# Output stage of a streaming encoder step: matmuls taken by tile and piece, and another order of column groups for the first tile

## The chip, the cores and the metric

One core of a Trainium2 chip runs the whole kernel. The metric is the device time of one execution in microseconds (us), lower is better. The engines are named as the profile names them: PE is TensorE (matmuls), PEld its weight loads, DVE is VectorE, ACT is ScalarE, POOL is GpSimd, SP is SyncE, whose queue issues nearly all DMA transfers. Each engine works through its own list of instructions in the order of that list.

## The reference, cut to what matters

The kernel computes one layer for 1024 prompt rows and 64 sample rows, 1024 columns wide, all in 32-bit floats: a normalised projection, eight heads of forgetting attention, four heads of attention to memory tokens, a pooling mixer, gates on all three, one output projection, and a last normalisation. The change concerns the last three steps alone:

```python
    cat = jnp.concatenate([
        jax.nn.silu(gf) * fox_o.reshape(B, S, FOX_W),
        jax.nn.silu(gp) * pool_o,
        jax.nn.silu(gm) * mem_o.reshape(B, S, MEM_W)], axis=-1)
    return x + cat @ w_out
...
    y_prompt = rmsnorm(hp, g_final)
    y_sample = rmsnorm(hs, g_final)
```

`cat` has 1024 columns, `w_out` is 1024 x 1024. The row norm at the end needs all 1024 columns of a row before any of them can be scaled.

## The kernel before, in words

**Two-part numbers.** Every product is built from 32-bit operands that are split in a high and a low part: high times high, high times low, low times high. So a product over 1024 rows of `w_out` is 8 steps of 128 rows (k = 0 to 7) with three matmuls each, 24 in all. For the 64 sample rows the high and the low part of `cat` lie side by side in one 128-column stationary operand, so a product takes 16 matmuls there, and the upper half of its result is added on afterwards (the copy `ysl`).

**Tiles and pieces.** The output stage goes over nine row tiles in the order `order = (8, 0, 1, ..., 7)` (line 1213): first the 64 sample rows (t = 8, here "the first tile"), then the prompt rows in tiles of 128. For each tile `out_prep(t)` (line 1150) loads the attention results and the gates, multiplies them and splits the product into `chi` (ACT) and `clo` (DVE); it does so in two halves, k = 0 to 3 and k = 4 to 7, for the prompt tiles. `out_tile(t)` (line 1248) then multiplies by the columns of `w_out` in three column groups: group 0 is columns 0 to 511, group 1 is 512 to 767, group 2 is 768 to 1023. One piece is one tile by one group: a run of 24 (or 16) matmuls, 512 or 256 columns wide. Groups 1 and 2 share one accumulator, so the three pieces fill two banks. The list `steps` (lines 1260 to 1263) gives the order in which the pieces are written down; two pieces that share an accumulator stay in that order, a piece in the other accumulator may pass them. When an accumulator is full, DVE adds the input rows `xt` to it, ACT squares the sum and adds it up, and after the second one DVE and ACT work out the row norm, scale the row and store it. The last tile (t = 7) uses three accumulators and does this per piece.

**Accumulators and buffers.** The tiles take the four PSUM rings in turn (line 1268): the first tile has `pp`, t = 0 has `s`, t = 1 has `pt`, t = 2 has `o`, t = 3 again `pp`, and so on up to t = 6 with `o` and t = 7 with `pp` and, for its third piece, `s`. In the trace the accumulator's name therefore tells the tile. `chi` and `clo` have room for three tiles in all, and two of the three places are those of the weights of the last projections. `xt` has two buffers: the third tile's rows are loaded when the first tile's rows have been stored.

**W_out.** `load_wout` (line 1219) brings the groups in the order 1, 0, 2, because it puts them where the three chunks of the normalised input lay, and these come free in that order as the last projections end. Each group is loaded, copied to a high part `wh` (ACT) and a rest `wl` (DVE or POOL), in two steps for a group of 256 columns and four for group 0.

**The order of the work.** All operations are first written down in a list with what they depend on. A planner (`Planner.flush`, line 190) then runs through them with a cost for each: at every step it takes, per engine, the operation with the smallest key of line 219,

```python
                    key = (t + late, op.rank, -op.level, op.seq)
```

where `t` is the earliest time at which that operation can start by the planner's own clock, `rank` is 0 for the output stage's matmuls, and `level` is the length of the longest chain of work that hangs on it. The result is the fixed list of each engine. Once several operations of PE can start at once, `rank` decides and then `level`; between tiles whose levels run close together the choice goes back and forth. All instructions are issued from line 252, so the trace is read by tile names and not by lines.

Of the kernel before, what the change touches and what calls it, by code (L numbers as in the profile page):

```python
# [42 lines left out]
class Planner:  # L43
# [5 lines left out]
    def __init__(self, nc, tc):  # L49
        self.nc, self.tc = nc, tc  # L50
        self.ops = []
        self.acc = {}
        self.slots = {}
        self.alloc = {}
        self.users = {}
        self.home = {}
        self.free = {e: 0.0 for e in self.ENG}
        self.lock = {"vector": 0.0, "gpsimd": 0.0}
        self.mode = self.table = None
        self.calm = self.boost = False  # L60
        self.dma = [0.0] * 16
        for e in self.ENG:
            setattr(self, e, _Eng(self, e))
# [31 lines left out]
    def add(self, eng, fn, args, kw):  # L95
        op = Op()
        op.eng, op.fn, op.args, op.kw = eng, fn, args, kw
        op.seq, op.succ, op.npred, op.ready, op.level = len(self.ops), [], 0, 0.0, 0.0
        op.mode = op.table = op.start = op.bytes = None
        op.port = False  # L100
        aps = [(i == 0, a) for i, a in enumerate(args)] + [(k in self.OUTS, a) for k, a in kw.items()]
        aps = [(w, a) for w, a in aps if hasattr(a, "tensor")]
        writes = [a for w, a in aps if w]
        reads = [a for w, a in aps if not w]
        self.cost(op, writes, reads)
        homes = {self.home.get(a.tensor.name) for a in writes + reads}
        into = {self.home.get(a.tensor.name) for a in writes}
        urgent = into & {"ps", "pt", "po"} if eng == "tensor" else "pp" in homes or "wp" in into
        op.rank = -1 if self.boost or urgent and not self.calm else 0
        preds = set()  # L110
        for w, a in aps:
            name, p0, p1, f0, f1 = self.box(a)
            hist = self.acc.setdefault(name, [])
            keep = []
            for h in hist:
                hw, q0, q1, g0, g1, o = h
                hit = q0 <= p1 and p0 <= q1 and g0 <= f1 and f0 <= g1
                if hit and (w or hw) and o is not op:
                    preds.add(o)
                if not (w and hit and p0 <= q0 and q1 <= p1 and f0 <= g0 and g1 <= f1) or o is op:  # L120
                    keep.append(h)
            keep.append((w, p0, p1, f0, f1, op))
            self.acc[name] = keep
            self.users.setdefault(name, []).append(op)
        for o in preds:
            self.link(o, op)
        self.ops.append(op)
        return op
# [144 lines left out]
def tile_hymba_step(  # L273
# [6 lines left out]
    nc = Planner(tc.nc, tc)  # L280
# [16 lines left out]
    def nm(s):  # L297
        uid[0] += 1
        return f"{s}_{uid[0]}"
# [10 lines left out]
    def row(name):  # L310
        return rp.tile([P, 512], F32, tag="row", name=nm(name))
# [65 lines left out]
    def quarter_ms(out, ss):  # L377
        nc.vector.tensor_scalar(out, ss, 0.25 / D, 0.25 * EPS, op0=ALU.mult, op1=ALU.add)

    def rsqrt(out, ms, pool):  # L380
        m, n = ms.shape
        t = pool.tile([P, 4], F32, tag="rsb", name=nm("rt"))[:m, :n]
        nc.scalar.activation(t, ms, AF.Sqrt)
        nc.vector.reciprocal(out, t)
        if n == 1:
            nc.vector.scalar_tensor_tensor(out, out, ms, t, op0=ALU.mult, op1=ALU.add)
        else:
            nc.vector.tensor_tensor(out, out, ms, op=ALU.mult)
            nc.vector.tensor_tensor(out, out, t, op=ALU.add)
        nc.vector.reciprocal(out, out)  # L390
# [41 lines left out]
    def mm3(acc, trip, n):  # L432
        for i, (l, r) in enumerate(trip):
            mm(acc, l, r, i == 0, i == n - 1)
# [378 lines left out]
    def small(shape, tag):  # L813
        return ap_.tile(shape, F32, tag=tag, name=nm(tag), bufs=6)
# [23 lines left out]
    def nbt(n):  # L838
        tag, w = ("nb", 512) if n <= 512 else ("nc", NPR)
        return ap_.tile([P, w], F32, tag=tag, name=nm(tag))  # L840

    def ptile(n=1024):
        tag, w, bufs = ("P", 512, 4) if n <= 512 else ("Q", 1024, 3)
        return ap_.tile([P, w], F32, tag=tag, name=nm(tag), bufs=bufs)
# [368 lines left out]
    order = (8, 0, 1, 2, 3, 4, 5, 6, 7)  # L1213
# [34 lines left out]
    def out_tile(t):  # L1248
        m = P if t < 8 else NSA
        c = slice(t * P, t * P + m)  # L1250
        if t not in prep:
            prep[t] = out_prep(t)
        xt_ = ap_.tile([P, NT + PAST], F32, tag="ks", name=nm("xt"))[:, :D]
        nc.sync.dma_start(xt_[:m], xn[c, :])
        xt = [xt_[:, :512], xt_[:, 512:]]
        ch, cl = prep[t]
        end = t == order[-1]
        ss = small([P, 4], "ss")
        xg = ptile() if end else None
        if end:  # L1260
            steps = [(0, 0, 0, 512, True), (1, 1, 0, 256, True), (2, 2, 0, 256, True)]
        else:
            steps = [(1, 2, 256, 256, False), (0, 0, 0, 512, True), (1, 1, 0, 256, True)]
        accs = {}
        prev = None
        for pi, pc, o, w, full in steps:
            if pi not in accs:
                ring = (ppt, pst, ptt, otile)[order.index(t) % 4]
                accs[pi] = ring() if pi < 2 else (pst if ring is ppt else ppt)()
            acc = accs[pi]  # L1270
            trip = []
            for k in range(KT):
                trip += [(ch[:, k, :], whi[pc][:, k, :w]), (ch[:, k, :], wlo[pc][:, k, :w])]
                if t < 8:
                    trip.append((cl[:, k, :], whi[pc][:, k, :w]))
            mm3(acc[:, o : o + w], trip, len(trip))
            if not full:
                continue
            n = w if end else 512
            c0 = (0, 512, 768)[pi]  # L1280
            x_ = xt[min(pi, 1)][:m, (0, 0, 256)[pi] : (0, 0, 256)[pi] + n]
            if t == 8:
                tt_ = row("ysl")
                nc.scalar.copy(tt_[:m], acc[m:, :])
                nc.vector.tensor_tensor(x_, tt_[:m], x_, op=ALU.add)
            nc.vector.tensor_tensor(x_, acc[:m, :n], x_, op=ALU.add)
            sp_ = ss[:m, pi : pi + 1]
            sq = nbt(512)
            nc.scalar.activation(sq[:m, :n], x_, AF.Square, accum_out=sp_)
            if prev is None:  # L1290
                quarter_ms(sp_, sp_)
            else:
                nc.vector.scalar_tensor_tensor(
                    sp_, sp_, 0.25 / D, prev, op0=ALU.mult, op1=ALU.add
                )
            prev = sp_
            if end:
                nc.vector.tensor_tensor(xg[:, c0 : c0 + n], x_, gfb[0][:m, c0 : c0 + n], op=ALU.mult)
        r = small([P, 1], "fr")
        rsqrt(r[:m], ss[:m, pi : pi + 1], ap_)  # L1300
        for nh in (0, 1):
            cols = slice(nh * 512, nh * 512 + 512)
            if not end:
                nc.vector.scalar_tensor_tensor(
                    xt[nh][:m], xt[nh][:m], r[:m], gfb[0][:m, cols], op0=ALU.mult, op1=ALU.mult
                )
                nc.sync.dma_start(y_o[c, cols], xt[nh][:m])
            elif nh:
                nc.vector.tensor_scalar(xg[:, cols], xg[:, cols], r, None, op0=ALU.mult)
                nc.sync.dma_start(y_o[c, cols], xg[:, cols])  # L1310
            else:
                nc.scalar.activation(xg[:, cols], xg[:, cols], AF.Copy, scale=r)
                nc.scalar.dma_start(y_o[c, cols], xg[:, cols])
# [64 lines left out]
    for t in order:  # L1378
        out_tile(t)
# [109 lines left out]
```

## Time and profile before

| what | value |
|---|---|
| median of 3 runs | 590.33 us (590.27 to 591.16) |
| the profiled execution's own time | 590.34 us |
| span of that execution, first to last instruction | 588.5 us |
| mean granted clock of TensorE | 0.996 of full speed |
| PE busy | 561.2 us (95% of the span), 3623 matmuls |
| DVE, ACT, POOL busy | 349.1, 299.1 and 249.8 us (59%, 51% and 42%) |
| DMA | 126.33 MB, mean 215 GB/s |

The span is what the trace covers; 1.84 us of the execution's own time lie outside it. Busy shares are means over stages with different limits. The output stage is the last 112 us or so of the span.

### The profile page before, as it was taken

Reading aid. Unit: us, or ns where it says so; the run is one execution under the profiler, and the core shown is the slowest. Engines: PE = TensorE matmul, PEld = TensorE weight load, DVE = VectorE, ACT = ScalarE, POOL = GpSimd, SP = SyncE. Lnnn points to the kernel's source line nnn. Section 1 sums busy time; section 2 is a strip of 40 time slices with the busy share of each in tenths; the row PEclk is TensorE's granted clock in tenths of the full one; section 3 lists DMA queues with packets and bytes.
Section 4 is the critical chain, followed back from the end, with each engine's and each line's share of the span. In section 5 each row is a group of like instructions: output and inputs, shape, how many; then the busy total and the mean of one; then the engine's idle time right before and its main releaser. Section 6 shows DMA issues by size and latency. Waiting matters only on the chain.

```text
span 588.5 us, 10778 instructions
## 1 busy us (share of the span) xinstructions
PE 561.2 (95%) x3623; PEld 504.3 (86%) x3623; DVE 349.1 (59%) x822; ACT 299.1 (51%) x675; POOL 249.8 (42%) x358
## 2 busy tenths in 40 slices
PE   7799999999999999999999999999999989999993
PEld 5789999888979889988988889889898867989983
DVE  5774431112788877756798965864356374656334
ACT  5564631121677877767886864862234243323202
POOL 2301464353774544434479851522323394322200
PEclk9999999999999999999999999999999999999998
DMA  8998753658997896596687897735256337577541
GB/s 301 312 339 298 229 174 117 242 202 281 281 349 242 291 280 189 154 322 210 213 238 269 274 263 235 210 125 152 76 152 187 113 109 195 142 231 213 159 143 72
DMA packets 96448, 126.33 MB, mean 215 GB/s; under 512 B 30434, under 2 KB 68618, under 8 KB 94858
## 3 DMA queue, kind: packets, MB, share of 16 engines
q1 hardware_dynamic: 96106, 125.39, 66.6%
q8 instruction: 29, 0.48, 0.3%
q10 hardware_dynamic: 288, 0.27, 0.1%
q14 instruction: 25, 0.20, 0.1%
HBM read 86.41 MB, written 39.21 MB: 213 GB/s over the span
## 4 chain that ended last, share of the span: by engine, by line
PE 76%; DMA 10%; DVE 6%; issue 3%; POOL 3%; ACT 1%; SPq 0%; DVEq 0%; POOLq 0%; ACTq 0%
PE pp L252 40%; PE s L252 13%; PE o L252 11%; PE pt L252 11%; DMA nat<-in_xn_dram 5%; POOL wl L252 2%; DMA nc<-gpd 2%; DMA nc<-gsd 1%; DMA catd<-cat 1%; DVE s L252 1%; DMA xr<-in_xT_dram 1%; DVE Q L252 1%; DVE ot L252 1%; DVE phl L252 1%; SPq L252 0%
## 5 line engine op out<-in xcount | busy, mean ns | idle before, releaser
L252 PE MATMUL pp<-xh,whi 128*128 128x320 f32 (+2 forms) x480 | 149.9, 335 | 2.8 <-DVE gr L252 1.1
L252 PE MATMUL pp<-xl,whi 128*128 128x320 f32 (+2 forms) x480 | 148.0, 331 | 0.0
L252 PE MATMUL pp<-xh,wlo 128*128 128x512 f32 (+2 forms) x480 | 147.7, 332 | 0.0
L252 PEld LDWEIGHTS pp<-xh,whi 128*128 128x128 f32 x480 | 88.1, 188 | 11.6 <-DVE gr L252 2.3
L252 POOL TENSOR_TENSOR wlo<-wr,whi 128x512 fp32r<-128x512 f32 (+2 forms) x44 | 60.1, 1384 | 86.7 <-ACT whi L252 75.1
L252 PEld LDWEIGHTS pp<-xh,wlo 128*128 128x128 f32 x480 | 88.1, 188 | 6.9
L252 PEld LDWEIGHTS pp<-xl,whi 128*128 128x128 f32 x480 | 88.1, 188 | 6.5
L252 DVE TENSOR_TENSOR phl<-pt,phl 128x512 fp32r<-128x512 f32 (+1 forms) x96 | 60.4, 642 | 11.9 <-ACT phl L252 10.8
L252 ACT CAST phl<-pt 128x512 fp32r<-128x512 f32 (+1 forms) x96 | 51.8, 550 | 25.0 <-PE pt L252 18.4
L252 POOL TENSOR_TENSOR cat<-ot 64x256 f32<-64x256 f32 x48 | 36.1, 754 | 55.6 <-DVE ot L252 33.0
L252 PE MATMUL o<-phl,vs 128*128 128x512 f32 (+1 forms) x160 | 55.3, 416 | 0.0
L252 PE MATMUL pt<-ident,Q 128*128 128x128 f32 x248 | 47.6, 272 | 1.9 <-DVE phl L252 1.8
L252 ACT CAST whi<-wr 128x1024 fp32r<-128x1024 f32 (+1 forms) x25 | 24.6, 982 | 45.2 <-PE pp L252 43.0
L252 ACT ACTIVATE Q<-Q,m 128x576 f32<-128x576 f32 (+4 forms) x40 | 38.0, 950 | 17.4 <-DVE m L252 17.1
L252 DVE TENSOR_TENSOR ot<-o,ot 64x512 f32<-64x512 f32 x48 | 32.8, 685 | 13.4 <-ACT ot L252 12.8
L252 PEld LDWEIGHTS pt<-ident,Q 128*128 128x128 f32 x248 | 32.1, 140 | 7.2 <-issue 2.2
L252 PE MATMUL s<-ks,qb 128*128 128x512 f32 (+3 forms) x128 | 37.4, 374 | 0.0
L252 POOL TENSOR_TENSOR P<-P,P 128x512 f32<-128x512 f32 (+2 forms) x17 | 18.5, 1096 | 41.8 <-DMA P<-catd 23.3
L252 ACT COPY ot<-o 64x512 f32<-64x512 f32 x48 | 27.9, 581 | 11.8 <-PE o L252 9.1
L252 PEld LDWEIGHTS o<-phl,vs 128*128 128x128 f32 x160 | 27.8, 190 | 3.3 <-DVE ot L252 0.2
L252 DVE CUSTOM_DVE_ANT_0 Q<-s,nc 128x512 f32<-128x512 f32 (+2 forms) x40 | 24.0, 599 | 10.9 <-PE s L252 6.0
L252 DVE TENSOR_TENSOR gr<-pp,rb 128x512 f32<-128x512 f32 (+2 forms) x24 | 12.5, 532 | 26.8 <-PE pp L252 25.8
(250 smaller groups left out, 1330.2 us busy)
## 6 DMA issues: line engine op xcount, KB each, us to landing
qd<-hl SPq DMA_DIRECT2D x24, 576.0 KB, 4.7
wr<-in_wt_dram SPq DMA_DIRECT2D x20, 512.0 KB, 4.2
qa<-qd SPq DMA_DIRECT2D x12, 640.0 KB, 5.7
ks<-kd SPq DMA_DIRECT2D x8, 800.0 KB, 6.4
qb<-qd SPq DMA_DIRECT2D x12, 512.0 KB, 5.0
P<-catd SPq DMA_DIRECT2D x17, 256.0 KB, 3.0
nat<-in_xn_dram SPq DMA_DIRECT2D x8, 512.0 KB, 8.1
kd<-hl SPq DMA_DIRECT2D x16, 256.0 KB, 5.1
```

The source lines that it names most:

```text
L252: getattr(getattr(self.nc, op.eng), op.fn)(*op.args, **op.kw)
```

## The change

Every operation of PE that `out_tile` writes down gets as its rank three times the place of its tile in the order, plus the place of its piece in `steps`. The rank stands ahead of the level in the planner's key, and behind the time. Ranks of other engines and of the earlier stages stay as they are. Besides, the first tile gets its own list of pieces: group 1, then group 0, then group 2, where it had 2, 0, 1 as the other tiles have.

```diff
         self.calm = self.boost = False
+        self.turn = None
...
         op.rank = -1 if self.boost or urgent and not self.calm else 0
+        if self.turn is not None and eng == "tensor":
+            op.rank = self.turn
...
         if end:
             steps = [(0, 0, 0, 512, True), (1, 1, 0, 256, True), (2, 2, 0, 256, True)]
+        elif t == order[0]:
+            steps = [(1, 1, 0, 256, False), (0, 0, 0, 512, True), (1, 2, 256, 256, True)]
         else:
             steps = [(1, 2, 256, 256, False), (0, 0, 0, 512, True), (1, 1, 0, 256, True)]
...
-        for pi, pc, o, w, full in steps:
+        for si, (pi, pc, o, w, full) in enumerate(steps):
+            nc.turn = 3 * order.index(t) + si
```

A step is (accumulator, column group, first column in the accumulator, width, whether the accumulator is full after it). Nothing is added to or taken from what is computed.

## Rows read from the trace of the kernel before

**Rows 1.** The profile's page, the chain of work that ended last: shares of the span by engine.

```profile
PE 76%; DMA 10%; DVE 6%; issue 3%; POOL 3%; ACT 1%; SPq 0%; DVEq 0%; POOLq 0%; ACTq 0%
```

**Rows 2.** Busy time by stretch of the span. Columns: stretch, its length, busy us (and instructions) of PE, PEld, DVE, ACT, POOL, granted clock of PE, DMA share, GB/s.

```profile
476.00:488.50 12.50, 8.47 (x33) 5.33 (x31) 8.62 (x12) 4.75 (x8) 11.20 (x10) 1.00 0.45 145
488.50:579.00 90.50, 90.49 (x594) 82.47 (x594) 44.41 (x95) 22.82 (x55) 21.66 (x28) 1.00 0.57 168
579.00:588.50 9.50, 0.00 (x0) 0.00 (x0) 5.12 (x20) 2.79 (x11) 0.00 (x0) 0.74 0.30 110
```

**Rows 3.** PE's timeline from the end of the last projection on. Columns: start us, duration us, engine, operation, accumulator and operands, shape, count, and in brackets the idle time before it and what ended it.

```profile
476.55 0.50 PE L252 MATMUL s<-wh,chi 128*128 128x512 f32 x1 [0.43 <-ACT chi L252]
...
478.31 0.50 PE L252 MATMUL s<-wh,clo 128*128 128x512 f32 x1 [1.02 <-DVE clo L252]
...
479.11 0.39 PE L252 MATMUL pp<-wh,chi 128*128 128x512 f32 x1
...
483.51 0.50 PE L252 MATMUL pp<-wl,chi 128*128 128x512 f32 x1 [0.56 <-POOL wl L252]
...
484.92 0.50 PE L252 MATMUL pp<-wl,chi 128*128 128x512 f32 x1 [0.69 <-POOL wl L252]
...
487.55 0.50 PE L252 MATMUL pt<-wh,chi 128*128 128x512 f32 x1 [1.20 <-ACT chi L252]
```

**Rows 4.** The timelines of DVE, POOL and ACT in the same stretch: when the parts of W_out and of the first tiles' operands were made.

```profile
461.29 2.89 POOL L252 TENSOR_TENSOR wl<-nc,wh 128x512 fp32r<-128x512 f32 x2 [4.31 <-ACT wh L252]
...
478.17 0.68 DVE L252 SCALAR_TENSOR_TENSOR chi<-P,chi 128x512 fp32r<-128x512 f32 x1
...
481.73 3.14 POOL L252 TENSOR_TENSOR wl<-wr,wh 128x512 fp32r<-128x512 f32 x2
...
486.38 0.58 ACT L252 COPY ysl<-pp 64x512 f32<-64x512 f32 x1 [6.50 <-PE pp L252]
486.87 0.63 ACT L252 ACTIVATE chi<-P 128x512 fp32r<-128x512 f32 x1
...
491.21 1.22 DVE L252 TENSOR_TENSOR wl<-wr,wh 128x1024 fp32r<-128x1024 f32 x1 [0.24 <-ACT wh L252]
```

**Rows 5.** PE's timeline where the matmuls run without a gap: two 512 wide on one accumulator, the first and the last of eleven 256 wide on one accumulator, and two 256 wide on alternating accumulators with 17 others between them.

```profile
480.92 0.40 PE L252 MATMUL s<-wh,clo 128*128 128x512 f32 x1
481.15 0.40 PE L252 MATMUL s<-wh,chi 128*128 128x512 f32 x1
...
493.18 0.28 PE L252 MATMUL pp<-wh,chi 128*128 128x256 f32 x1
...
494.38 0.28 PE L252 MATMUL pp<-wh,chi 128*128 128x256 f32 x1
...
500.07 0.28 PE L252 MATMUL s<-wh,clo 128*128 128x256 f32 x1
...
502.17 0.28 PE L252 MATMUL s<-wh,clo 128*128 128x256 f32 x1
```

**Rows 6.** All engines at the end of the span, in order of time: the last matmuls of t = 6 (`o`) and of t = 7 (`s`), and the work behind them up to the last stores.

```profile
577.54 0.28 PE L252 MATMUL o<-wh,clo 128*128 128x256 f32 x1
...
578.71 0.28 PE L252 MATMUL s<-wh,clo 128*128 128x256 f32 x1
...
579.40 0.41 DVE L252 TENSOR_TENSOR xt<-s,xt 128x256 f32<-128x256 f32 x1
...
580.28 0.40 ACT L252 ACTIVATE nb<-xt 128x256 f32<-128x256 f32 x1
580.59 0.19 ACT L252 ACTIVATION_READ_ACCUMULATOR nb<-xt 128x1 f32 x1
...
581.12 0.15 DVE L252 SCALAR_TENSOR_TENSOR ss<-ss 128x1 f32<-128x1 f32 x1
...
581.31 0.20 ACT L252 ACTIVATE rt<-ss 128x1 f32<-128x1 f32 x1 [0.44 <-DVE ss L252]
...
581.86 0.15 DVE L252 RECIPROCAL fr<-rt 128x1 f32<-128x1 f32 x1
...
582.30 0.22 DVE L252 RECIPROCAL fr<-fr 128x1 f32<-128x1 f32 x2
582.50 0.72 ACT L252 ACTIVATE Q<-Q,fr 128x512 f32<-128x512 f32 x1 [0.99 <-DVE fr L252]
582.56 1.42 DVE L252 SCALAR_TENSOR_TENSOR xt<-xt,fr,gfb 128x512 f32<-128x512 f32 x2
...
583.89 0.48 DVE L252 TENSOR_SCALAR Q<-Q,fr 128x512 f32<-128x512 f32 x1
584.40 0.62 SPq L252 DMA_DIRECT2D out_dram<-Q  x1
```

**Rows 7.** Two of the last stretches of the span, columns as in rows 2: the first in which the last stores moved data, and the one in which nothing moved any more.

```profile
584.00:584.40 0.40, 0.00 (x0) 0.00 (x0) 0.38 (x1) 0.00 (x0) 0.00 (x0) 0.50 0.63 241
...
587.20:588.50 1.30, 0.00 (x0) 0.00 (x0) 0.00 (x0) 0.00 (x0) 0.00 (x0) 0.50 0.00 0
```

**Rows 8.** ACT and DVE in the middle of the stage: the first tile's second evacuation, the second half of t = 2's operands, and DVE's wait for the input rows of t = 1, whose releaser is the store of the first tile's rows out of the same buffer.

```profile
499.62 0.59 ACT L252 COPY ysl<-pp 64x512 f32<-64x512 f32 x1 [2.65 <-PE pp L252]
...
509.38 0.69 DVE L252 SCALAR_TENSOR_TENSOR clo<-P,chi 128x512 fp32r<-128x512 f32 x1 [0.37 <-ACT chi L252]
...
516.80 1.29 DVE L252 TENSOR_TENSOR xt<-pt,xt 128x512 f32<-128x512 f32 x2 [3.19 <-DMA out_dram<-xt]
```

## The prediction, made before the changed kernel was run

> **What bounds the kernel now.** I read the views from the coarse to the fine. The chain of work that ended last says that PE is the engine to look at: 76% of the span [rows 1]. The busy time by stretch says where in the output stage PE is not the limit. From 488.5 to 579.0 us it is busy for 90.49 of 90.50 us, at a granted clock of 1.00, which is the 2.4 GHz level; there only fewer matmuls would help. Before that, from 476.0 to 488.5, it is busy for 8.47 of 12.50 us, so 4.03 us are idle. After it, from 579.0 to 588.5, it does nothing for 9.5 us [rows 2]. The reader is to keep these two holes in mind, 4.0 and 9.5 us, since an order of matmuls can change only them.
>
> The PE timeline shows what fills the first hole. PE starts on `s` (t = 0) at 476.55, waits 1.02 us for `clo`, begins the first tile (`pp`) at 479.11, and then waits for the rest of group 0 of W_out (`wl`, 0.56 and 0.69 us) and 1.20 us for the operands of t = 1 [rows 3]. All of these matmuls are 512 wide: group 0. The timelines of the helpers say why no other group is used. Group 1 is complete at 464.18 (461.29 + 2.89), group 0 only at 484.87, group 2 at 492.44 [rows 4]. But group 1 stands behind group 2 in `steps`, in the same accumulator, so what was ready first waits for what comes last.
>
> The timeline of all engines shows the second hole: t = 6 (`o`) ends at 577.54 + 0.28 = 577.82 and t = 7 at 578.71 + 0.28 = 578.99, only 1.2 us later [rows 6]. Both evacuations then stand on DVE and ACT at once, with PE idle.
>
> **Part 1: the first tile takes group 1 first.** It adds and removes no instruction. It moves 16 matmuls of 256 columns from behind 492.44 into the first hole. One such matmul follows another after 0.12 us (493.18 to 494.38 is ten steps); on alternating accumulators it is (502.17 - 500.07) / 18 = 0.117 us, so changing accumulators costs nothing and saves nothing [rows 5]. 16 x 0.1175 = 1.9 us. The first tile's operand is ready at 478.17 + 0.68 = 478.85 [rows 4]. From there to 487.55, where t = 1 begins, are 8.7 us. Work to be placed there: 16 matmuls of the first tile on group 0 and the 7 of t = 0 that are left of its first twelve, each 0.23 us (480.92 to 481.15) [rows 5], which is 5.4 us, and now 1.9 us more: 7.3 of 8.7. So it fits. It can't all fall where PE idles today: the first tile's last matmuls still wait for `wl` at 484.87, and PE keeps the planned order, so up to 0.7 us (the wait at 484.92 [rows 3]) may be lost to a matmul of `s` planned on the wrong side of a wait. The bounds are 1.2 and 1.9 us; I take 1.9, since by rank the seven of `s` come behind the first tile and so fill exactly its waits.
> Behind 487.55 the supply is as it was: the second half of t = 0, then group 2 at 492.44. No wait on W_out is added, since group 2 now stands third, not first, for the first tile. ACT's `ysl` at 486.38 and the `chi` behind it at 486.87 [rows 4] keep their place, as group 0 ends when it did.
>
> **Part 2: matmuls by tile and piece.** Again no instruction comes or goes, on PE or on a DMA queue: weight loads are one per matmul in both orders. Each prompt tile now runs as one block: 24 x 0.23 + 48 x 0.1175 = 11.2 us. In the full stretch this changes nothing by itself. At the end, t = 6 is finished 11.2 us before the last matmul, and the first two pieces of t = 7 are finished 5.6 and 2.8 us before it, so their evacuation lies beside matmuls. What is left after the last matmul is one piece of 256 columns. From the durations and the start distances of [rows 6], with 0.04 us from PE to DVE or between DVE and ACT and 0.07 us into the square: add 0.04 + 0.41, square and its accumulator 0.07 + 0.50, `ss` 0.04 + 0.15, root 0.04 + 0.20, then to the last reciprocal 0.04 + 0.44 (581.86 to 582.30) and to the scaling 0.20 (582.30 to 582.50): 2.13 us, and then DVE's half 0.48 and ACT's half 0.72 side by side. The product with `gfb` (0.4 us on DVE) fits beside the square. So SP's last store is issued at 2.64 us after the last matmul and ACT's at 2.85, where today SP's goes out at 584.40, which is 5.41 us after it [rows 6]. The reason is in the same rows: today the two scalings of t = 6 (582.56, 1.42 us) stand before that of t = 7, and their adds and sums before its.
> From the last issue to the end of the span it takes 588.5 - 584.40 = 4.1 us today. Data moves from about 584.1 to 587, and nothing in the last 1.3 us [rows 7]: four stores of 256 KB (128 x 512 x 4 bytes) in 2.8 us. With two stores left it is 1.4 us of data. One bound keeps the 4.1 us: a tail of 2.85 + 4.1 = 7.0 us, 2.5 saved. The other takes 0.8 us from issue to first data, 1.4 us of data and 1.5 us to the end: 2.64 + 3.7 = 6.4, 3.1 saved. I take the middle, 2.8 us, since some of the 4.1 us is the queue of the other two stores, but not all.
>
> **The cover that strict order gives up.** Mixed tiles always have other matmuls at hand; in strict order a late operand stops PE. The nearest place is t = 2: its second half's `clo` is finished at 509.38 + 0.69 = 510.07 today [rows 8]. In strict order, group 2 is complete at 492.44, then follow the rest of t = 0 on group 0, the first tile's group 2 (ending near 495.7), two pieces of t = 0 and the three of t = 1 less the half done at 491: t = 2 starts near 509.7 and needs k = 4 at 511.1. The first tile leaves PE at 495.7 instead of 499.6 [rows 8], which frees its operand's place and its evacuation 3.9 us sooner, so that `clo` should come near 506. Slack 5 us; later tiles have 22 us for each preparation. Cost taken: 0; bounds 0 and 4.2 us per boundary (next part).
> The trace shows mixing as full cover, 0.01 us idle in 90.5 [rows 2]. The Trainium skill, page "Perfetto Trace Analysis", section "Optimization Strategy", says that where the contended engine changes over time, interleaving the regimes may help; by it, un-mixing is the wrong direction, and the rival right below gives the time. In this stage the contended engine is PE in all tiles alike, so the trace bears it out only for the two holes.
>
> **Sum.** 590.34 - 1.9 - 2.8 = 585.6 us against the profiled execution's own time; the median, 590.33, is the same number. Its own range: 585.0 (2.0 and 3.3 saved) to 586.6 (1.2 and 2.5).
>
> **Rivals.**
> *DVE holds the operands back (slower).* The first tile's store must be done before t = 1's input rows are loaded into its `xt`; today DVE waits 3.19 us for that, until 516.80, at the add for t = 1 [rows 8]. Strict order finishes the first accumulator of t = 1 near 507, while the rows come only 3.9 us sooner, near 512.9. If the planner, whose clock differs from the chip's, put that add ahead of t = 2's `clo`, this would be ready at 512.9 + 1.3 + 0.7 = 514.9 or later, 3.8 to 4.2 us after PE wants it. One such stall gives 590.34 - 4.7 + 4.2 = 589.8, no change; two, at t = 2 and at t = 3, give 590.34 - 4.7 + 8.4 = 594.0. It decides from 4.7 us of idle PE between 488.5 and the last matmul. For it: the wait exists today. Against it: the planner counts that load too, and it orders by when things are ready.
> *The first hole stays.* The planner's clock has the first tile's operand later than the chip, so `s` goes first and the new matmuls end behind 487.55: only the tail's 2.8 us, 587.5.
> *The tail stays long.* The last two tiles part, but the end hangs on stores and on small operations in the same order: 0.5 us instead of 2.8 saved at the end, 587.9. Against it: SP's last store can't wait for t = 6 any more.
> *It doesn't do what it says.* If matmuls are ready one at a time, `t` decides and rank never does: 590.3. Against it: 594 matmuls in 90.5 us without a gap, so many are ready at once [rows 2].
>
> **How the numbers follow.** Forecast 0.64; first hole stays 0.12; tail stays long 0.09; one stall or no effect 0.07; two stalls or more 0.08. A change below 0.2% (1.2 us) can't be told from none here. Faster: 0.64 + 0.12 + 0.09 = 0.85; same 0.07; slower 0.08. The range goes from 584.7, a little below the forecast's own lower end for what the sums leave out, to 588.6, which takes in the second and third rival.
>
> **What would show it.** Right: between 476 and 488.5 PE is busy about 10.3 us instead of 8.47, with `pp` 256 wide right after 479; in the full stretch runs of 24 on one accumulator, and no idle; the last `o` 11 us before the last matmul; about 6.7 us from that matmul to the end of the span. Wrong: idle PE at a change of tile with `clo` or `chi` as its releaser, DVE waiting for `xt` longer than 3.2 us, or a last store issued later than 3.5 us after the last matmul.

## The result, and the profile after

The changed kernel takes 584.55 us, the median of 3 runs (584.19 to 586.34), beside 590.33 us before: a ratio of 0.9914 with a 95% interval of 0.9888 to 0.994. The forecast was 585.6 us in a range of 584.7 to 588.6: the median lies 0.15 us below the lower end, while the ratio, taken of 590.33, gives 585.3 us, inside it. The span of the profiled execution is 582.8 us, against 588.5.

Busy time by stretch of the changed kernel, columns as in [rows 2]:

```profile
476.00:488.50 12.50, 10.24 (x51) 8.08 (x51) 7.76 (x9) 4.43 (x9) 10.17 (x9) 1.00 0.48 143
488.50:573.00 84.50, 84.50 (x549) 76.77 (x548) 49.42 (x103) 23.56 (x58) 21.69 (x27) 1.00 0.62 183
573.00:582.80 9.80, 3.20 (x28) 3.00 (x26) 3.05 (x10) 1.95 (x6) 0.00 (x0) 0.91 0.14 54
```

In the first 12.5 us PE is busy for 10.24 us where [rows 2] had 8.47. Part of that is the window: the stage begins 1.26 us earlier here, and in a window moved by as much (474.74 to 487.24) PE is busy for 9.81 us. The long stretch is still without a gap. The last stretch holds the end of PE's work and what follows it. PE's timeline, which answers to [rows 3], shows what fills the first hole:

```profile
475.29 0.51 PE L255 MATMUL s<-wh,chi 128*128 128x512 f32 x1 [0.42 <-ACT chi L255]
...
477.04 0.50 PE L255 MATMUL s<-wh,clo 128*128 128x512 f32 x1 [1.01 <-DVE clo L255]
...
477.83 0.28 PE L255 MATMUL pp<-wh,chi 128*128 128x256 f32 x1
...
479.62 0.28 PE L255 MATMUL pp<-wl,chi 128*128 128x256 f32 x1
...
486.43 0.50 PE L255 MATMUL pt<-wh,chi 128*128 128x512 f32 x1 [1.20 <-ACT chi L255]
```

Sixteen `pp` matmuls of 256 columns stand where the first tile used to begin with group 0, and the two waits for `wl` (0.56 and 0.69 us) are gone. The wait for `chi` of t = 1 stays at 1.20 us. The chain of waits (start, length, what) then shows each tile as one block of 72 matmuls, 11.2 to 11.3 us, and at the end 24 matmuls of the last piece:

```profile
508.61 11.29 PE o L255 x72
519.90 11.28 PE pp L255 x72
...
553.67 11.29 PE o L255 x72
564.95 8.43 PE pp L255 x48
573.38 2.84 PE s L255 x24
```

The last `o` (t = 6) now ends at 553.67 + 11.29 = 564.96, 11.2 us before the last matmul; in [rows 6] it was 1.2 us. The timeline of all engines behind the last matmul, which answers to [rows 6]:

```profile
575.92 0.28 PE L255 MATMUL s<-wh,clo 128*128 128x256 f32 x1
576.24 0.42 DVE L255 TENSOR_TENSOR xt<-s,xt 128x256 f32<-128x256 f32 x1 [1.60 <-PE s L255]
...
576.76 0.42 ACT L255 ACTIVATE nb<-xt 128x256 f32<-128x256 f32 x1 [2.31 <-DVE xt L255]
...
578.38 0.72 ACT L255 ACTIVATE Q<-Q,fr 128x512 f32<-128x512 f32 x1 [0.68 <-DVE fr L255]
578.38 0.49 DVE L255 TENSOR_SCALAR Q<-Q,fr 128x512 f32<-128x512 f32 x1
578.90 0.33 SPq L255 DMA_DIRECT2D out_dram<-Q  x1
579.13 0.35 ACTq L255 DMA_DIRECT2D out_dram<-Q  x1
```

PE ends at 575.92 + 0.28 = 576.20. Nothing of t = 6 stands between the steps of t = 7 any more: SP's last store goes out 2.70 us after the last matmul (5.41 before), and the span ends 6.60 us after it (9.51 before).

**Where the span's 5.7 us went.** The first column is the start of the first `s` matmul, the second the time from there to the end of the last matmul, the third what is left of the span.

| profile | stage begins | to the last matmul's end | tail |
|---|---|---|---|
| before | 476.55 | 102.44 | 9.51 |
| after | 475.29 | 100.91 | 6.60 |
| difference | 1.26 | 1.53 | 2.91 |

The last two columns are the change. The first is not explained by it: up to the first `s` matmul both kernels carry out the same 2999 matmuls, 699 operations of DVE, 604 of ACT and 323 of POOL, on each engine in the same order by operation and tile name. The experiments come back to it.

### The profile page after: what moved, and what is told of

It is laid out like the page before. It is cut to its first block, busy times and chain, and to the rows that moved or that the text cites. A ratio compares the mean times of both kernels' runs of the same rounds, so it can differ in the third digit from the quotient of the medians.

```text
span 582.8 us, 10769 instructions
## 1 busy us (share of the span) xinstructions
PE 561.7 (96%) x3623; PEld 506.3 (87%) x3623; DVE 352.6 (60%) x822; ACT 299.8 (51%) x675; POOL 250.2 (43%) x358
## 4 chain that ended last, share of the span: by engine, by line
PE 82%; DMA 7%; DVE 6%; issue 2%; ACT 2%; SPq 1%; POOL 0%; ACTq 0%; DVEq 0%; POOLq 0%
PE pp L255 44%; PE s L255 15%; PE o L255 12%; PE pt L255 11%; DMA nat<-in_xn_dram 2%; DMA xr<-in_xT_dram 1%; DMA nc<-gsd 1%; DMA kd<-hl 1%; DMA wr<-in_wv_dram 1%; DVE s L255 1%; SPq L255 1%; DMA catd<-cat 1%; DVE phl L255 1%; DVE gmg L255 1%; DVE ot L255 0%
## 5 line engine op out<-in xcount | busy, mean ns | idle before, releaser
L255 ACT ACTIVATE nb<-xt 128x512 f32<-128x512 f32 (+2 forms) x19 | 11.5, 606 | 43.7 <-DVE xt L255 42.1
```

Source lines behind the costliest of these rows:

```text
L255: getattr(getattr(self.nc, op.eng), op.fn)(*op.args, **op.kw)
```

## The experiments

The theory from the two profiles: there are two holes, each closed by its own edit, and the order within the full stretch is worth nothing. The rivals: the ranks alone do it all; strict order costs cover somewhere and what was seen is a remainder; or the gain is only a better last two tiles. Each ratio below is to runs of the kernel before that were made beside it.

**The ranks alone.** The first tile's own list goes.

```diff
-        elif t == order[0]:
-            steps = [(1, 1, 0, 256, False), (0, 0, 0, 512, True), (1, 2, 256, 256, True)]
```

> The ranks of the change alone; the first tile keeps its old list of pieces (group 2, 0, 1). Two holes, each closed by its own edit (my theory): the tail is 6.6 us as in the changed kernel, but the 16 matmuls on group 1 still run behind group 2, so the wait for the first operands of t = 1 is as before: 590.3 - 2.9 = 587.4 us. Rival, the ranks do it all: 584.6 us, no loss against the changed kernel.

Measured: 587.26 us (11 runs), before beside it 590.36, ratio 0.9959 (0.9943 to 0.9976), a gain of 3.1 us. The tail is 6.59 us, and the first hole is as it was before, with the waits for `wl` (0.56 us here, 0.68 at 483.33) and 1.20 us at 485.97 (a row at the end of this document, where the profile shows something else as well).

```profile
481.92 0.50 PE L255 MATMUL pp<-wl,chi 128*128 128x512 f32 x1 [0.56 <-POOL wl L255]
```

**The list alone.** The two lines that set the rank go.

```diff
-        if self.turn is not None and eng == "tensor":
-            op.rank = self.turn
```

> The new list of pieces of the first tile alone; no ranks, so tiles mix by level as before. Two holes: group 1 is used early, 1.9 us saved, and the tail stays at 9.5 us with both last tiles behind the last matmul: 588.4 us. Rival, the new list works only with the ranks (by level other matmuls go first): 590.3 us.

Measured: 588.08 us (12 runs), ratio 0.9963 (0.9946 to 0.998), a gain of 2.3 us. From the stage's begin at 476.23 to the last matmul's end at 576.90 it is 100.67 us, 1.8 less than before; the tail is 586.5 - 576.90 = 9.6 us, as long as before. PE has two waits left in the hole, 1.02 us for `clo` of t = 0 and this one:

```profile
487.38 0.50 PE L253 MATMUL pt<-wh,chi 128*128 128x512 f32 x1 [1.20 <-ACT chi L253]
```

So each edit closes one hole and leaves the other: by stage, the list alone gives 1.8 us of the first and the ranks alone 9.51 - 6.59 = 2.9 us of the second. The gains of the medians, 3.1 + 2.3 = 5.4 us, add up to what both give together (5.5 to 5.8), but they also hold what the stage's begin scatters by (below). The rival by which the ranks do it all falls.

**Strict order for the last two tiles only.**

```diff
-            nc.turn = 3 * order.index(t) + si
+            nc.turn = max(0, 3 * (order.index(t) - 7) + si + 1) if order.index(t) > 6 else 0
```

> The changed kernel with ranks for the last two tiles (t = 6 and t = 7) only; the first seven tiles mix by level as before. Two holes: strict order in the full stretch is worth nothing, the same time as the changed kernel within 0.5 us (585.0), tail 6.6 us. Rival, strict order also feeds PE better or worse in the middle: 1 us or more away from the changed kernel.

Measured: 585.05 us (6 runs), ratio 0.9919 (0.9901 to 0.9938). The tail is 7.29 us and not the 6.6 expected. DVE's timeline says why. The adds for t = 6 wait 3.60 us for their input rows. In DVE's list the row norm of t = 6 then stands behind the first two adds of t = 7 (570.80 and 573.62), before which DVE waits 4.86 and 2.14 us for PE. So one scaling of t = 6 begins just before the last matmul's end (576.41) and the other one behind it.

```profile
564.64 1.29 DVE L255 TENSOR_TENSOR xt<-o,xt 128x512 f32<-128x512 f32 x2 [3.60 <-DMA xt<-in_xn_dram]
...
576.09 0.75 DVE L255 SCALAR_TENSOR_TENSOR xt<-xt,fr,gfb 128x512 f32<-128x512 f32 x1
577.55 0.74 DVE L255 SCALAR_TENSOR_TENSOR xt<-xt,fr,gfb 128x512 f32<-128x512 f32 x1
```

Two scalings of t = 6, 0.75 and 0.74 us, stand among the steps of t = 7 once more. The time from begin to last matmul, 576.41 - 475.60 = 100.81, is 0.1 us less than that of after (100.91): un-mixing the tiles in the middle gains nothing by itself. With the middle mixed the end is less clean, by 0.7 us of tail.

**By tile, not by piece.**

```diff
-            nc.turn = 3 * order.index(t) + si
+            nc.turn = 3 * order.index(t)
```

> The changed kernel with a rank by tile, the same for its three pieces, which then mix by level. Two holes: the first two pieces of t = 7 end together with the third, so two adds (0.69 and 0.41 us) and two squares more stand behind the last matmul: tail 7.8 to 8.3 us instead of 6.6, time 586 to 586.5. Rival, only the parting of t = 6 and t = 7 counts and DVE and ACT take the pieces side by side: within 0.3 us of the changed kernel.

Measured: 586.84 us (6 runs), ratio 0.9943 (0.9923 to 0.9963), with a tail of 586.2 - 578.72 = 7.5 us. Both are misses: the time is above the 586 to 586.5 us expected, the tail below the 7.8 to 8.3. The profiled execution (587.97 us, the slowest of the six) began its stage at 477.90, later than any other changed kernel, so the tail says more than the time. Of t = 7, two pieces end in the last 0.2 us of PE's work and the first about 0.8 us before (DVE adds to it from 577.93 on), and their evacuation comes last. The tail says the pieces are worth 0.9 us of the 2.9 and the tiles 2.0.

**After, unedited, and before, unedited: how far does the stage's begin scatter?**

> The changed kernel again, unedited, for a tighter interval beside the others of this call. Two holes: 1.9 us at the start and 2.9 us at the end, so 585.5 us, ratio 0.992. Rival, the changed order also shortens the stages ahead of it (they were 1.2 us shorter in its first profile): 584.3 us, and the first matmul of t = 0 at 475.3 us again instead of scattering from profile to profile.

> The kernel before, unedited, for a second profile. Theory (the 1.26 us by which the output stage began earlier in the first profile of after is scatter of the start): the first matmul of s begins anywhere between 474.9 and 477.9, as it did over the profiles of the changed kernels; from there to the first matmul of pt 11.0 us; from there to the last matmul 91.4 us; 9.5 us behind it. Rival (the change brings the stage forward): it begins after 476.5 again, later than in most of the changed ones.

Measured: after 584.55 us (6 runs; before beside it 590.03; 0.9907, 0.9885 to 0.9928), before 589.42 us (10 runs; 0.9989 to itself, 0.9965 to 1.0013). The second profile of before begins the stage later, with the same waits as in [rows 3]:

```profile
478.23 0.50 PE L252 MATMUL s<-wh,chi 128*128 128x512 f32 x1 [0.43 <-ACT chi L252]
...
485.20 0.50 PE L252 MATMUL pp<-wl,chi 128*128 128x512 f32 x1 [0.56 <-POOL wl L252]
```

| profile | stage begins | to the last matmul's end | tail |
|---|---|---|---|
| before, first and second | 476.55, 478.23 | 102.44, 102.46 | 9.51, 9.61 |
| after, first and second | 475.29, 474.94 | 100.91, 100.92 | 6.60, 6.54 |

The last two columns repeat to 0.1 us; the first differs by 1.7 us for one and the same kernel, and over all profiles of this study it lies between 474.94 and 478.23. What the change is worth is therefore 1.54 + 2.99 = 4.5 us. The medians differ by 5.5 us, and the interval of the ratio, 4.2 to 6.8 us of 590.03, takes in the 4.5. On this both expectations came out nearer to their rival: the time of after is nearer to 584.3 than to 585.5 us, and before began at 478.23, later than the 474.9 to 477.9 that the theory gave. The traces show no way for it, though. The change has no order to act through ahead of the stage, since the operations there and their order are the same. And in the first pair 0.90 of the 1.26 us is there already at 39 us of the span, where PE has waited 1.47 us for DVE before the change and 0.46 us after it. Both begins of before lie above both of after, but a changed kernel with the same work ahead of the stage (by tile) began at 477.90. Whether the last 1 us of the medians is that scatter alone isn't settled, since only the profiled executions show where their stage began.

**Group 1 first for every tile but the last.** The changed kernel, with the list 1, 0, 2 for these eight tiles (t = 7 keeps its own).

```diff
-        elif t == order[0]:
+        else:
             steps = [(1, 1, 0, 256, False), (0, 0, 0, 512, True), (1, 2, 256, 256, True)]
-        else:
-            steps = [(1, 2, 256, 256, False), (0, 0, 0, 512, True), (1, 1, 0, 256, True)]
```

> The changed kernel with the list 1, 0, 2 for all tiles but the last. Two holes: t = 0 can now use group 1 for its first half as well (12 matmuls, 1.4 us) in the 1.2 us wait for the first operands of t = 1, so up to 1.2 us less than the changed kernel, 584.3 us. Rival, the wait is set by ACT (its copy of the first tile's result stands before the operand) and PE's end of group 0 comes later by what is put ahead of it: no gain, 585.5 us.

Measured: 584.06 us (6 runs), ratio 0.9896 (0.9874 to 0.9918). The profile shows the wait for `chi` of t = 1 filled: `s` matmuls run to 486.40, and `pt` follows with no wait.

```profile
486.44 0.38 PE L255 MATMUL pt<-wh,chi 128*128 128x256 f32 x1
```

From the begin to the last matmul it is 574.56 - 475.23 = 99.33 us, 1.6 us less than after; 0.2 us of it is a shorter wait for `clo` of t = 0 (0.80 us). Timed, it is 0.5 us ahead of after, within what this measurement can tell. The same kernel with `ysl` copied by DVE instead of ACT, so that `chi` doesn't stand behind it:

```diff
-                nc.scalar.copy(tt_[:m], acc[m:, :])
+                nc.vector.tensor_copy(tt_[:m], acc[m:, :])
```

> As the one before, and the copy of the first tile's lower half (ysl) goes to DVE instead of ACT. Two holes: the operand of t = 1 no longer waits on ACT behind that copy (0.85 us), so the first hole shrinks by up to 0.85 us more: 583.5 us. Rival, DVE takes over the wait, since clo of t = 1 stands behind the copy there: 584.3 us or the same as the kernel before it.

Measured: 584.03 us (5 runs), ratio 0.9896 (0.9872 to 0.992): nothing more. DVE has taken over the wait, as the rival said: `clo` of t = 1 now comes 0.53 us late for PE, and from the begin to the last matmul it is 575.70 - 476.01 = 99.69 us.

```profile
488.39 0.39 PE L255 MATMUL pt<-wh,clo 128*128 128x256 f32 x1 [0.53 <-DVE clo L255]
```

**Two places for the operands instead of three, in strict and in mixed order.** This takes away preparation ahead, on which strict order would have to lean. In mixed order the two lines that set the rank go as well, as in the list alone.

```diff
-        spare = order.index(t) % 3 == 2
+        spare = False
```

> The changed kernel with room for the operands of two tiles instead of three, so those of a tile can only be made once the tile two before it has left PE (11.2 us ahead). Strict order needs one tile running and one prepared: two holes only, 585.5 to 586 us, no idle PE in the full stretch. Rival, strict order has no cover and a preparation takes as long as a tile (the nearest operand came 0.5 us before its use with three places): PE idles at the changes of tile, 590 us or more.

> After without the ranks and with two places for the operands instead of three, so mixed tiles with less preparation ahead. Beside strict order with two places (586.73) it asks what mixing is worth as cover. Theory (what two places cost is the fill at the start of the stage, where there is little to mix, and mixing hides nothing later): about 588.1 + 2.2 = 590.3, with the idle time of PE in the first 25 us of the stage and the long tail of 9.5 us. Rival (mixed tiles always have other matmuls at hand): the places cost nothing, 588.1.

Measured: strict 586.73 us (9 runs; 590.03 beside it; 0.9953, 0.9934 to 0.9972), mixed 590.8 us (10 runs; 590.65 beside it; 0.9998, 0.9973 to 1.0022). Against the same order with three places (584.55 and 588.08) that is 2.2 and 2.7 us more; strict order is 0.7 us above the 585.5 to 586 expected and well below the rival's 590. All waits of PE in the stage, in strict order with two places:

```profile
475.83 0.50 PE L255 MATMUL s<-wh,chi 128*128 128x512 f32 x1 [1.87 <-ACT chi L255]
485.14 0.50 PE L255 MATMUL s<-wh,chi 128*128 128x512 f32 x1 [0.62 <-ACT chi L255]
486.27 0.50 PE L255 MATMUL s<-wh,clo 128*128 128x512 f32 x1 [0.39 <-DVE clo L255]
489.34 0.39 PE L255 MATMUL pp<-wh,chi 128*128 128x256 f32 x1 [0.49 <-ACT wh L255]
490.77 0.38 PE L255 MATMUL pp<-wl,chi 128*128 128x256 f32 x1 [0.92 <-DVE wl L255]
```

and its busy time afterwards:

```profile
500.00:577.00 77.00, 77.00 (x490) 69.65 (x489) 42.79 (x92) 18.38 (x47) 17.84 (x24) 1.00 0.58 180
```

PE's waits are all in the first 15 us; which of them the missing place causes is not shown one by one, and two end on parts of W_out. From 500 us on PE doesn't wait once, with even less preparation ahead. Mixed order loses as much, with waits of 1.79, 0.98 and 1.22 us up to 493.03 and none of 0.1 us behind that, so mixing was no cover that strict order lacks. (Its profile also holds a stretch at a lower clock, shown in the last section.)

## Why the prediction came out right, point by point

**The two holes** were the right reading: each edit closed the hole it was assigned to, shown by the two kernels with one edit each. The sum is right in its terms and near in size: by stage the change gives 1.5 + 3.0 = 4.5 us where 4.7 was forecast. Part of that nearness is luck, since the first part was put 0.4 us too high and the second 0.2 us too low. The 1 us more by which the medians differ (5.5 and 5.8) belongs to neither part, and the forecast had no term for it.

**Part 1** was put at 1.9 us (bounds 1.2 and 1.9); the two pairs of profiles show 102.45 - 100.915 = 1.54 us. The count was right: between the begin of the stage and the first `pt` PE now issues the 12 matmuls of `s` and the 16 of `pp` that it issued before, and 16 of 256 columns more, which took 477.83 to 479.75, 1.92 us. Two things were missed.

The first is how much room the hole had. The sum put 7.3 us of work into 8.7 us, but the last 1.2 us of these are the wait for `chi` of t = 1. ACT makes that behind `ysl`, which waits for the first tile's last matmul on group 0 [rows 4], so nothing placed ahead of that matmul can fill it. The room was what the two waits for `wl` cost. Where 0.23 us would do, the matmul that waited came 0.95 and 1.07 us after the one before it (482.56 to 483.51, 483.85 to 484.92), and the next one 0.34 us after that: 1.8 us in all, a little less than 1.92. So the first tile's last matmul on group 0 comes 484.84 - 475.29 = 9.55 us after the stage's begin where it came 485.96 - 476.55 = 9.41, and the hole is 11.14 us long where it was 11.00. The rows, before and after:

```profile
485.96 0.39 PE L252 MATMUL pp<-wl,chi 128*128 128x512 f32 x1
...
484.84 0.39 PE L255 MATMUL pp<-wl,chi 128*128 128x512 f32 x1
```

The second is that strict order isn't quite free in the full stretch. From the first `pt` to the last matmul's end the step leaves 91.44 - 1.92 = 89.52 us. The list alone takes just that, 576.90 - 487.38 = 89.52. The changed kernel takes 89.77 us (89.76 in its second profile), and with strict order for the last two tiles only it is 89.63. No wait stands in the 0.25 us; they are spread over the matmuls, and their cause is not traced.

**Part 2** was put at 2.8 us; measured 2.99 over both pairs. Step by step: SP's store 2.64 us after the last matmul (2.70 measured), ACT's 2.85 (579.13 - 576.20 = 2.93), from there to the end 4.1 at most (582.8 - 579.13 = 3.67 us). The gain lies nearer to the bound of 3.1: with four stores at the end it is 4.1 us from the last issue to the end of the span (4.2 with the list alone, 586.5 - 582.31), with two 3.67 us (3.65 by tile, 586.2 - 582.55).

**The cover** was costed at nothing, and no wait came of it (the 0.25 us above are no wait), but the margin behind that was wrong. The step "`clo` should come near 506 ... Slack 5 us; later tiles have 22 us" failed. DVE's timeline after the change:

```profile
507.56 0.68 DVE L255 SCALAR_TENSOR_TENSOR clo<-P,chi 128x512 fp32r<-128x512 f32 x1
...
512.71 0.69 DVE L255 TENSOR_TENSOR P<-P,rt 128x512 f32<-128x512 f32 x1 [4.47 <-DMA P<-catd]
513.96 1.29 DVE L255 TENSOR_TENSOR xt<-pt,xt 128x512 f32<-128x512 f32 x2 [0.56 <-DMA xt<-in_xn_dram]
...
519.65 1.29 DVE L255 SCALAR_TENSOR_TENSOR clo<-P,chi 128x512 fp32r<-128x512 f32 x2
```

The second half of t = 2 is ready at 508.24 and PE takes it at 511.05: 2.8 us of slack. For t = 3 it is less. DVE waits 4.47 us for a load and then makes the first half of t = 4 before the second half of t = 3; the ranks of the change order PE's work alone. The latter is ready at 520.94, over one microsecond after t = 3 begins on PE. PE's list takes it late here: between the matmuls of 256 columns the planner, whose key puts time ahead of rank, set some of group 0, 512 wide.

```profile
521.05 0.28 PE L255 MATMUL pp<-wh,clo 128*128 128x256 f32 x1
521.16 0.39 PE L255 MATMUL pp<-wh,chi 128*128 128x512 f32 x1
...
522.56 0.51 PE L255 MATMUL pp<-wh,clo 128*128 128x512 f32 x2
```

The fourth `clo` step of 256 columns is at 521.05; the fifth, the first that needs the second half, is the other one in the pair at 522.56, near 522.8: 1.9 us of slack. A strict block would have wanted it three matmuls of 0.12 us after 521.05, at 521.4, with 0.5 us of slack. So the order "by tile and piece" is not blind, though here a strict block would have held too. At t = 6 the slack is smaller still: the second half is ready at 552.89 + 0.69 = 553.58 at the earliest, and PE takes it at 555.16, so 1.6 us at most.

```profile
552.89 0.69 DVE L255 SCALAR_TENSOR_TENSOR clo<-P,chi 128x512 fp32r<-128x512 f32 x1 [0.37 <-ACT chi L255]
...
555.16 0.28 PE L255 MATMUL o<-wh,clo 128*128 128x256 f32 x1
```

**The rivals.** The slower rival needed the add for t = 1 ahead of `clo` of t = 2 in DVE's list. It stands behind it (513.96 and 507.56 in the rows above). The input rows came no sooner than the rival had them, near 513.9 where 512.9 was worked out; that DVE's wait for `xt` is 0.56 us instead of 3.19 is because it waited 4.47 us for another load first. No PE wait appears between 487.3 and 576.2 us: the rival's condition, 4.7 us of idle PE, is nowhere met. "The first hole stays" and "the tail stays long" are refuted by the rows above, and the kernels with one edit each show what they would have given: 587.26 against the 587.5 worked out, and 588.08 against 587.9. That the change does nothing falls with the blocks of 72.

The Trainium skill, page "Perfetto Trace Analysis", section "Optimization Strategy", says that where the most-contended engine changes over time, interleaving those regimes may help. Here PE is busy for all of 84.50 us of the full stretch, so there was no second regime to interleave with, and un-mixing the middle cost 0.1 us (100.91 against 100.81). No run here tests the rule itself.

## What to carry to other kernels

Where one engine is busy without a gap, an order changes mainly the two ends of that stretch (in between it was 0.25 us here): ask what is ready first at its start, and how much is left to do when its last operation ends. Tiles whose work runs side by side are ready together; give the last one a finish of its own, in pieces, and let the one before it be done by then. And split a difference between two profiles by stage before believing it: 1.3 of the 5.7 us here were the begin of a stage that the change doesn't touch.

## What the hardware showed that was not expected

In the profile with the ranks alone, PE's granted clock fell to half, the 1.2 GHz level, right behind the first hole. Busy time by stretch, columns as in [rows 2]:

```profile
480.00:482.00 2.00, 1.44 (x7) 0.83 (x5) 2.00 (x2) 0.00 (x0) 2.00 (x3) 1.00 0.00 0
482.00:484.00 2.00, 1.32 (x5) 0.80 (x6) 0.14 (x1) 0.00 (x0) 2.00 (x2) 1.00 0.00 0
484.00:486.00 2.00, 0.80 (x5) 0.32 (x3) 0.59 (x1) 1.11 (x2) 2.00 (x4) 1.00 0.75 244
486.00:488.00 2.00, 2.00 (x5) 1.41 (x6) 1.38 (x3) 0.59 (x2) 1.10 (x1) 0.51 0.96 240
488.00:490.00 2.00, 2.00 (x8) 1.57 (x7) 1.22 (x3) 1.59 (x4) 0.00 (x0) 0.64 1.14 268
```

PE's timeline of the same profile shows what that does to matmuls of one shape:

```profile
485.97 0.75 PE L255 MATMUL pt<-wh,chi 128*128 128x512 f32 x1 [1.20 <-ACT chi L255]
...
487.42 0.63 PE L255 MATMUL pt<-wh,chi 128*128 128x512 f32 x1
487.85 0.63 PE L255 MATMUL pt<-wl,chi 128*128 128x512 f32 x1
...
489.76 0.39 PE L255 MATMUL pt<-wh,chi 128*128 128x512 f32 x1
489.99 0.40 PE L255 MATMUL pt<-wl,chi 128*128 128x512 f32 x1
```

PE was busy for 1.44, 1.32 and 0.80 us of three stretches of 2 us; behind them one 512-wide matmul follows another after 0.43 us (487.42 to 487.85), and after 0.23 us again from 489.52 on (489.76 to 489.99). From the begin of the stage to its last matmul this profile takes 578.91 - 474.96 = 103.95 us, 1.5 more than before with the same hole; strict order accounts for 0.25 of that. The first profile of before was busy for 1.44, 1.31 and 0.80 us in three such stretches (482 to 488) and kept a clock of 1.00, as the second did, so the hole doesn't always cost it. A second profile, mixed order with two places, showed the same after a wait of 1.79 us ahead of the stage, while strict order with two places kept 1.00 after 1.87 us there:

```profile
476.00:478.00 2.00, 0.70 (x2) 0.61 (x3) 2.00 (x4) 1.69 (x4) 1.01 (x1) 0.86 0.52 196
478.00:480.00 2.00, 2.00 (x10) 1.90 (x10) 0.83 (x3) 1.43 (x2) 1.44 (x2) 0.50 0.54 159
480.00:482.00 2.00, 2.00 (x13) 1.86 (x13) 1.47 (x2) 0.00 (x0) 2.00 (x2) 0.78 0.36 108
```

None of the other ten profiles has it in the output stage before the last matmul. So filling a hole may now and then save more than the idle time itself; that is not shown, and how often the clock falls is not known from twelve profiles.
